# Down weights of a Strassen group stored by column half, loaded in four pieces instead of two

## The chip, the cores and the metric

The kernel runs on one core of a Trainium2 chip. The metric is the device time of one execution in microseconds (us); smaller is better. All arrays are float32, and TensorE multiplies them as fp32r (a float32 number cut into a high and a low part, three products for one).

## The reference

The reference is a trunk of two layers on 512 tokens of width 1024. Layer 0 mixes tokens by causal pooling, layer 1 by stick-breaking attention; each is followed by the MLP below, and every branch is wrapped in RMS norms. The change touches the second matrix of the MLP only, `w_down` (4096 x 1024).

```python
def sq_relu_mlp(h, w_up, w_down):
    u = jnp.matmul(h, w_up)
    return jnp.matmul(jnp.square(jax.nn.relu(u)), w_down)

for layer in range(DEPTH):                      # DEPTH = 2, D_FF = 4096
    ...                                         # mixer, residual
    h = rms_norm(x, mlp_pre_g[layer])
    x = x + rms_norm(sq_relu_mlp(h, w_up[layer], w_down[layer]), mlp_post_g[layer])
```

## The kernel before

**The MLP in blocks.** The 4096 hidden channels are 32 blocks of 128 (`NJ`). For each block the up projection (`up_block`, lines 764, 767 and 768: 24 matmuls of 512 columns) fills one PSUM bank; ScalarE takes relu and square of it into SBUF (`up`, lines 673 and 674). The weights of an up block come by DMA into a tile `raw`, are split by ScalarE into a high part (line 190) and by VectorE into a low part (line 192), up to four blocks ahead.

**The down projection by Strassen groups.** 28 of the 32 blocks go through the class `Seven`: five groups per layer with `GROUPS` = 2, 3, 3, 3, 3 pairs of blocks. A group multiplies 2x2 block matrices with seven products instead of eight. Its weights are four quarters: `w11`, `w12` (first block of each pair, output columns 0 to 511 and 512 to 1023) and `w21`, `w22` (second block of each pair). They are loaded unsplit: `w11` and `w12` lie in a tile `w1` (in the profile `w<-in_wdn`), `w21` and `w22` in `xn3`, a tile of three rows of 1024 that the norms use outside the MLP (in the profile `xn<-in_wdn`). For each product, `make(i)` builds the two operands: `left` forms sums of activations (line 593, tiles `r` and `s`), `right` forms sums of weight quarters (line 612), and both are split into high and low parts in tiles `a` and `w` (helper `split`: ScalarE line 312, VectorE line 313). The weight operands are, in order of the products 0 to 6:

- `w11`; then `w22 - w12` (tile `e`); then `e + w11`; then `w21 - e`; then `w12 - w11` (written over `w12`); then `w21`; then `w22`.

So the first sum of a group needs `w22` and `w12`, `w21` is not read before product 3, and the last reader of a group's `w22` is the split for its product 6.

**Order of the work.** Operands are made two products ahead: in the step of product i, `make(i + 2)` is called, and in the last two steps the coming group's products 0 and 1. One up block of the coming group follows each product on TensorE (line 638 is a product's matmul: 6 per pair, so 18 for a group of three pairs). A scheduler orders each engine's instructions by a timeline of its own at build time; each engine and the DMA queue of SP then run their list in order. In layer 0 SP also carries the weights of the attention: `split_apart` loads a block (`apart` or `spare`, line 243), ScalarE scales and splits it (lines 202 and 252), and both parts are written back to DRAM (`kept`, line 233).

**The loads.** `load(0)` and `load(1)` (line 577) fetch both quarters of one tile each. In DRAM `wdn` is block after block, 128 rows of 1024 each, so one load reads, for each of the 128 partitions, n rows of 4 KB that lie 1 MB apart, and writes them one after another into the partition.

Of the kernel before, what the change touches and what calls it, by code (L numbers as in the profile page):

```python
# [10 lines left out]
F32 = mybir.dt.float32  # L11
# [4 lines left out]
P = 128  # L16
D = 1024
# [4 lines left out]
NJ = FF // P  # L22
GRP = 4

GROUPS = (2, 3, 3, 3, 3)
MOST = max(GROUPS)
HEADS = 16
HD = 64
PAIRS = HEADS // 2
WINDOWS = (2, 4, 8, 16)  # L30
# [3 lines left out]
NS = [slice(0, 512), slice(512, 1024)]  # L34
# [90 lines left out]
def trunk(ctx, tc, x, bands, grow, pw, wup, wdn, wq, wk, wv, wo, out):  # L125
    nc = tc.nc
# [11 lines left out]
    def name(s):  # L138
        uid[0] += 1
        return f"{s}{uid[0]}"  # L140
# [14 lines left out]
    xn3 = work.tile([P, 3, D], F32, tag="xn3", name="xn3")  # L155
# [39 lines left out]
    def gains(lo, n):  # L195


        def scaled(raw):
            m = max(n, 4)
            for k in range(m):  # L200
                c, at = raw[:, k * D // m : (k + 1) * D // m], lo + k * n // m
                nc.scalar.mul(c, c, gc[:, at : at + 1])  # L202

        return scaled
# [3 lines left out]
    def want(key, src, scaled=None):  # L208
        queue.append((key, src, scaled))
# [16 lines left out]
    apart, kept, going = [], {}, []  # L226
# [52 lines left out]
    for l in range(2):  # L279
        if l == 1:  # L280
            n = len(queue)
            for what, i, part in ATT_ORDER:
                if what == "H" and not i and 0 in part:
                    for h in range(4):
                        want(("v", 0, h), wv[h], gains(C_KV * KC + 2 * h, 2))
                elif what == "V" and 0 in part:
                    for h in range(2):
                        want(("v", i, h), wv[2 * i + h], gains(C_KV * KC + 4 * h, 4))
                elif what == "K":
                    want(("k", i), wk[i], gains(C_KV * KC, KC))  # L290
                elif what in "PQ":
                    if ("k", i) not in [k for k, _, _ in queue]:
                        want(("k", i), wk[i], gains(C_KV * KC, KC))
                    want(("q", i), wq[i], gains(C_MIX_PRE1 * KC, KC))
                elif what == "O" and 0 in part or what == "E":
                    for c in range(2 * i, 2 * i + 2 if what == "O" else PAIRS):
                        want(("o", c), wo[c])
            asked = {x[0]: x for x in queue[n:]}
            for what in SPLIT_ORDER:
                key = (what[0], *(int(c) for c in what[1:]))  # L300
                apart.append(asked.pop(key))
            assert sorted(asked) == [("o", 0), ("o", 1)]

            queue[n - GRP : n + GRP] = queue[n : n + GRP - 1] + queue[n - GRP : n] + queue[n + GRP - 1 : n + GRP]
        for j in range(NJ):
            want(("up", l, j), wup[l, j])
        for j in range(NJ - GRP, NJ):
            want(("dn", l, j), wdn[l, j])


    def split(src, hi, lo):
        latest["act"] = nc.scalar.copy(hi, src)  # L312
        latest["dve"] = nc.vector.tensor_tensor(out=lo, in0=src, in1=hi.bitcast(F32), op=ALU.subtract)  # L313
# [160 lines left out]
    def need(*tiles):  # L474
        for t in tiles:
            if t in pending:
                pending.pop(t).transpose()
# [68 lines left out]
    class Seven:  # L546
# [19 lines left out]
            self.l, self.first, self.n, self.mp = l, first, n, mp  # L566
            self.banks, self.written, self.operands = {}, None, {}

        def load(self, second):

            n = self.n
            if second:
                w = self.w2 = xn3
            else:
                w = self.w1 = self.mp.tile([P, MOST, D], F32, tag="w1", name=name("w1"))
            src = wdn[self.l, self.first : self.first + 2 * n].rearrange("(n k) p d -> k p n d", k=2)
            nc.sync.dma_start(w[:, :n], src[1 if second else 0])

        def squares(self):
            self.r = self.mp.tile([P, 2, MOST, S], F32, tag="r", bufs=2, name=name("r"))  # L580

# [3 lines left out]
        def left(self, i):  # L585
# [4 lines left out]
            if i == 0:  # L590
                self.s1 = self.mp.tile([P, MOST, S // 2], F32, tag="s1", name=name("s1"))
            s1 = self.s1[:, :n]
# [7 lines left out]
            src = {"r11": r11, "s3": r21, "s2": r11, "r22": r22, "s1": s1, "r12": r12, "s4": r11}[key]  # L600
            a = self.mp.tile([P, 2, MOST, S // 2], F32R, tag="a", bufs=2, name=name("a"))
            split(src, a[:, 0, :n], a[:, 1, :n])
            return a

        def right(self, i):

            n, key = self.n, self.PRODUCTS[i][2]
            w11, w12, w21, w22 = (w[:, :n, h] for w in (self.w1, self.w2) for h in NS)
            if i == 0:
                self.e = self.mp.tile([P, MOST, 512], F32, tag="e", name=name("e"))  # L610
            e = self.e[:, :n]
            combine = lambda out, x, y, op=ALU.subtract: nc.vector.tensor_tensor(out=out, in0=x, in1=y, op=op)  # L612
            if key == "t3":
                combine(e, w22, w12)
            elif key == "t2":
                combine(e, e, w11, ALU.add)
            elif key == "t4":
                combine(e, w21, e)
            elif key == "t1":
                combine(w12, w12, w11)  # L620
            src = {"w11": w11, "t3": e, "t2": e, "t4": e, "t1": w12, "w21": w21, "w22": w22}[key]
            w = self.mp.tile([P, 2, MOST, 512], F32R, tag="w", bufs=2, name=name("w"))
            split(src, w[:, 0, :n], w[:, 1, :n])
            return w
# [24 lines left out]
    def mlp(l, mp, update):  # L649
# [5 lines left out]
        groups = [Seven(l, firsts[g], n, mp) for g, n in enumerate(GROUPS)]  # L655
# [27 lines left out]
                squares.append((a[:, 0], a[:, 1]))  # L683

        entering = dict(normed_by)
        groups[0].load(0)
        groups[0].squares()
        if l == 0:
            apart_hi[0] = wts.tile([P, 2, D], F32R, tag="wx", name=name("wx"))
# [5 lines left out]
        for j, (pu, w) in enumerate(first):  # L695
            if j == n0 - 1:
                need(2, 3)
                groups[0].load(1)
            if j >= len(early):
                up_block(pu, w, slice(0, S // 2))  # L700
        early.clear()
# [8 lines left out]
        for g, group in enumerate(groups):  # L710
            coming = groups[g + 1] if g + 1 < len(groups) else None
            if coming:
                coming.squares()
            ups = list(range(firsts[g + 1], firsts[g + 1] + 2 * GROUPS[g + 1]) if coming else range(plain, NJ))
            if g == 0:
                up(ups.pop(0))
                fill()
            else:
                with tc.issue_after(latest["dve"].ins):
                    while entering:  # L720
                        entering.popitem()[1].homogeneous_eps()
            for i in range(7):
                group.product(i, y, written if g == 0 else None)
                if 7 * g + i in steps:
                    with tc.issue_after(latest["act"].ins), tc.issue_after(latest["dve"].ins):
                        split_apart(mp)
                if ups:
                    up(ups.pop(0))
                if i + 2 < 7:
                    group.make(i + 2)  # L730
                    if i + 2 == 4 and coming:
                        coming.load(0)
                    if i + 2 == 6 and coming:
                        coming.load(1)
                elif coming:
                    coming.make(i + 2 - 7)
                elif i == 5:
                    piece = lambda tag, k, bufs=1: mp.tile([P, k, D], F32R, tag=tag, bufs=bufs, name=name("dn"))
                    w, e, x = piece("w1", 3), piece("e", 1), piece("w", 3, 2)
                    c = piece("apart", 1, 3)[:, 0]  # L740
                    dn_raw["dn", l, NJ - 2] = mp.tile([P, D], F32, tag="apart", bufs=3, name=name("dn"))
                    dn_raw["dn", l, NJ - 1] = mp.tile([P, D], F32, tag="apart", bufs=3, name=name("dn"))
                    dn_pool[0] = [[w[:, 0], w[:, 1]], [w[:, 2], e[:, 0]], [c, x[:, 2]], [x[:, 0], x[:, 1]]]

                if l == 0:
                    behind.update(latest)
                fill(1 + (coming is None and i == 6))
# [3 lines left out]
        w = [get(("dn", l, j)) for j in range(plain, NJ)]  # L751
# [24 lines left out]
    with tc.tile_pool(name="mix0", bufs=1, reuse_waits="tile") as mp:  # L776
# [6 lines left out]
        half = NW * BW // 2  # L783
# [9 lines left out]
        at = D + P + 4 * KC  # L793
# [16 lines left out]
        left, stats, ups, ys, own = {}, {}, {}, {}, {}  # L810
# [146 lines left out]
    with tc.tile_pool(name="att", bufs=1, reuse_waits="tile") as ap:  # L957
# [68 lines left out]
        half = [slice(0, HD), slice(HD, P)]  # L1026
# [20 lines left out]
        with tc.issue_after(latest["pool"].ins):  # L1047
            nc.gpsimd.memset(begin, 0.0)
            for lo, n in SEG.values():
                c = min(n - P, 1)  # L1050
                d = begin[:, lo + n - P - c : lo + n]
# [320 lines left out]
    return np.concatenate([packed, *first], axis=1).astype(np.float32)  # L1372


# [43 lines left out]
```

## Time and profile before

The columns of a row of instruction groups on the profile's page are: line, engine, operation, output<-inputs, shape, count | busy time, mean of one | idle time before it and what ended it.

| what | before |
|---|---|
| median of three runs | 899.36 us (897.89, 899.36, 899.59) |
| the profiled execution | 899.84 us, of which 898.1 us are the profiled span |
| TensorE busy | 888.9 us (99% of the span) |
| VectorE, ScalarE busy | 690.4 us (77%), 555.6 us (62%) |
| granted TensorE clock, mean | 0.998 |
| loads of a group of three pairs (1.5 MB), layer 0, issue to landing | 7.8 to 11.2 us |
| the same, layer 1 | 6.7 to 7.1 us |

A matmul's row shows 0.38 us for 512 columns, but the next one starts 0.22 us later: they are pipelined, so TensorE is at its pace when the starts follow each other at 0.22 us. Idle time of an engine costs nothing unless it delays TensorE, which is what the span is made of.

### The profile page before, as it was taken

To read this page: it belongs to the slowest core of one execution; us is meant where nothing else is said; L and a number is where in the kernel's file an instruction comes from. 1 tells how busy PE (TensorE), PEld (TensorE's weight loads), DVE (VectorE), ACT (ScalarE), POOL (GpSimd) and SP (SyncE) were. 2 spreads that over 40 slices of the span, in tenths; PEclk is the share of its full clock that TensorE was granted. 3 is DMA by queue.
4 is the path that set the end of the run, shared out by engine and by line. 5 is a ranking of instruction groups with operands and counts; after the bars stand their busy time and mean duration, and the time that the engine had idled before them with its cause. 6 is when DMAs were issued, how large, how long until landed. Compare 5 with 4: busy or idle time off the path is not lost.

```text
span 898.1 us, 12323 instructions
## 1 busy us (share of the span) xinstructions
PE 888.9 (99%) x4688; PEld 786.5 (88%) x4688; DVE 690.4 (77%) x800; ACT 555.6 (62%) x984; POOL 37.8 (4%) x78
## 2 busy tenths in 40 slices
PE   9999999999999999999999999999999999999997
PEld 6998888888888888888999888998888888888886
DVE  6876799998988977268777478884696976968866
ACT  6667679898796947256455464875545444444632
POOL 3200000000000004000000000200000000000002
PEclk9999999999999999999999999999999999999999
DMA  8446969889698750643152272442514233133002
GB/s 303 147 148 217 344 233 340 326 277 410 220 342 285 285 189 2 209 166 134 56 187 93 95 281 71 153 176 96 186 40 164 79 140 117 47 141 118 24 1 94
DMA packets 42685, 155.73 MB, mean 173 GB/s; under 512 B 4225, under 2 KB 4353, under 8 KB 42626
## 3 DMA queue, kind: packets, MB, share of 16 engines
q1 hardware_dynamic: 42624, 154.94, 47.9%
q8 instruction: 37, 0.61, 0.3%
q14 instruction: 22, 0.18, 0.1%
q10 hardware_dynamic: 2, 0.00, 0.0%
HBM read 121.38 MB, written 33.55 MB: 173 GB/s over the span
## 4 chain that ended last, share of the span: by engine, by line
PE 87%; DVE 4%; DMA 4%; ACT 3%; issue 2%; POOL 0%; SPq 0%; POOLq 0%; ACTq 0%; DVEq 0%
PE ps L638 24%; PE ps L767 14%; PE ps L764 14%; PE ps L768 14%; PE ps L331 4%; PE ps L333 4%; PE ps L332 4%; DMA xn<-in_wdn 2%; PE ps L1133 2%; PE ps L1114 2%; PE ps L1158 2%; PE ps L903 1%; PE ps L438 1%; DVE w L313 1%; DMA x<-in_x 1%
## 5 line engine op out<-in xcount | busy, mean ns | idle before, releaser
L638 PE MATMUL ps<-w,a 128*128 128x512 f32 x1176 | 266.3, 379 | 0.7 <-ACT a L312 0.7
L767 PE MATMUL ps<-xnh,w 128*128 128x512 f32 (+1 forms) x704 | 253.4, 362 | 0.0
L768 PE MATMUL ps<-xnl,w 128*128 128x512 f32 (+1 forms) x704 | 252.8, 360 | 0.0
L764 PE MATMUL ps<-xnh,w 128*128 128x512 f32 (+1 forms) x704 | 252.2, 360 | 0.3 <-DVE w L924 0.3
L638 PEld LDWEIGHTS ps<-w,a 128*128 128x128 f32 x1176 | 222.0, 189 | 32.9 <-ACT a L312 1.1
L764 PEld LDWEIGHTS ps<-xnh,w 128*128 128x128 f32 x704 | 132.9, 190 | 15.9 <-DVE w L924 0.4
L768 PEld LDWEIGHTS ps<-xnl,w 128*128 128x128 f32 x704 | 133.5, 190 | 15.2
L767 PEld LDWEIGHTS ps<-xnh,w 128*128 128x128 f32 x704 | 133.0, 190 | 15.3
L192 DVE TENSOR_TENSOR w<-raw,w 128x1024 fp32r<-128x1024 f32 x58 | 70.8, 1221 | 48.4 <-ACT w L190 48.4
L190 ACT CAST w<-raw 128x1024 fp32r<-128x1024 f32 x58 | 60.6, 1044 | 69.2 <-PE ps L764 68.2
L647 DVE TENSOR_TENSOR y<-ps,y 128x512 f32<-128x512 f32 x124 | 83.7, 684 | 24.5 <-PE ps L638 24.2
L312 ACT CAST a<-r 128x768 fp32r<-128x768 f32 (+1 forms) x60 | 47.4, 790 | 56.0 <-PE ps L638 36.5
L312 ACT CAST w<-e 128x1536 fp32r<-128x1536 f32 (+1 forms) x30 | 41.8, 1392 | 34.3 <-DVE e L612 26.2
L313 DVE TENSOR_TENSOR a<-r,a 128x768 fp32r<-128x768 f32 (+1 forms) x60 | 53.9, 898 | 8.3 <-ACT a L312 8.3
L1095 DVE TENSOR_TENSOR_SCAN e<-u,begin 128x1280 f32<-128x1280 f32 x16 | 45.2, 2825 | 18.6 <-ACT u L1079 17.9
L313 DVE TENSOR_TENSOR w<-e,w 128x1536 fp32r<-128x1536 f32 (+1 forms) x30 | 49.3, 1644 | 0.7 <-ACT w L312 0.5
L202 ACT ACTIVATE apart<-apart,eye 128x128 f32<-128x128 f32 (+1 forms) x128 | 42.4, 409 | 0.0
L313 DVE TENSOR_TENSOR w<-w,w 128x1536 fp32r<-128x1536 f32 (+1 forms) x20 | 33.0, 1648 | 4.7 <-ACT w L312 4.7
L674 ACT ACTIVATE r<-r 128x512 f32<-128x512 f32 x56 | 35.3, 630 | 1.3
L313 DVE TENSOR_TENSOR w<-xn,w 128x1536 fp32r<-128x1536 f32 (+1 forms) x20 | 33.0, 1649 | 3.7 <-ACT w L312 3.3
L673 ACT ACTIVATE r<-ps 128x512 f32<-128x512 f32 x56 | 33.1, 591 | 3.9 <-PE ps L764 3.9
L312 ACT CAST w<-w 128x1536 fp32r<-128x1536 f32 (+1 forms) x20 | 27.7, 1385 | 5.9 <-DMA w<-in_wdn 5.9
(148 smaller groups left out, 1293.4 us busy)
## 6 DMA issues: line engine op xcount, KB each, us to landing
raw<-in_wup SPq DMA_DIRECT2D x64, 512.0 KB, 3.8
w<-kept SPq DMA_DIRECT2D x60, 512.0 KB, 4.3
kept<-wx SPq DMA_DIRECT2D x30, 512.0 KB, 5.2
kept<-apart SPq DMA_DIRECT2D x24, 512.0 KB, 5.9
w<-in_wdn SPq DMA_DIRECT2D x8, 1536.0 KB, 7.4
xn<-in_wdn SPq DMA_DIRECT2D x8, 1536.0 KB, 8.3
apart<-in_wq SPq DMA_DIRECT2D x7, 512.0 KB, 6.9
kept<-spare SPq DMA_DIRECT2D x6, 512.0 KB, 6.0
```

What stands on the lines that cost most here:

```text
L190: nc.scalar.copy(hi, raw)
L192: nc.vector.tensor_tensor(out=lo, in0=raw, in1=hi.bitcast(F32), op=ALU.subtract)
L202: nc.scalar.mul(c, c, gc[:, at : at + 1])
L312: latest["act"] = nc.scalar.copy(hi, src)
L313: latest["dve"] = nc.vector.tensor_tensor(out=lo, in0=src, in1=hi.bitcast(F32), op=ALU.subtract)
L331: nc.tensor.matmul(dst, ah, bh, start=start, stop=False)
L638: nc.tensor.matmul(bank, a[:, x, q, TS[t]], woven(w[:, z, q], NS[0]), start=start and q == 0 and k == 0, stop=q == self.n - 1 and k == 2, ...
L647: nc.vector.tensor_tensor(out=part, in0=bank, in1=part, op=ALU.add)
L764: nc.tensor.matmul(pu[:, cols], wl[:, k, :], moving(xnh, k), start=False, stop=k == KC - 1)
L767: nc.tensor.matmul(pu[:, cols], wh[:, k, :], moving(xnh, k), start=k == 0, stop=False)
L768: nc.tensor.matmul(pu[:, cols], wh[:, k, :], moving(xnl, k), start=False, stop=False)
L1095: nc.vector.tensor_tensor_scan(out=self.e[:, ::-1], data0=self.u[:, 1:][:, ::-1], data1=begin[:, ::-1], initial=0.0, op0=ALU.mult, op1=ALU ...
```

## The change

`wdn` is stored group by group as a flat array: for each group first `w11` of all its pairs, then `w12`, `w21`, `w22`; in each quarter the partition is outermost, so a partition's share of a quarter is n x 512 numbers in one piece (6 KB for three pairs, 4 KB for two), and a quarter of a group of three pairs is one piece of 0.75 MB. The two SBUF tiles get the same order: half 0 is numbers 0 to 1535 of a partition, half 1 is 1536 to 3071. `load(second, half)` fetches one quarter. The loads are asked for after the `make` of the steps 2, 3, 4 and 5: `w11`, `w12`, `w22`, `w21`. What is computed, and with which operations, is the same.

```diff
+LOADS = {2: (0, 0), 3: (0, 1), 4: (1, 1), 5: (1, 0)}
...
-        def load(self, second):
+        def load(self, second, half):
             n = self.n
             if second:
-                w = self.w2 = xn3
-            else:
-                w = self.w1 = self.mp.tile([P, MOST, D], F32, tag="w1", name=name("w1"))
-            src = wdn[self.l, self.first : self.first + 2 * n].rearrange("(n k) p d -> k p n d", k=2)
-            nc.sync.dma_start(w[:, :n], src[1 if second else 0])
+                self.w2 = xn3.rearrange("p n d -> p (n d)").rearrange("p (h n c) -> p h n c", h=2, n=MOST)
+            elif not half:
+                self.w1 = self.mp.tile([P, 2, MOST, 512], F32, tag="w1", name=name("w1"))
+            size = P * n * 512
+            src = wdn[self.l, self.first * P * D + (2 * second + half) * size :][: size]
+            w = self.w2 if second else self.w1
+            nc.sync.dma_start(w[:, half, :n], src.rearrange("(p n c) -> p n c", p=P, n=n))
...
-            w11, w12, w21, w22 = (w[:, :n, h] for w in (self.w1, self.w2) for h in NS)
+            w11, w12, w21, w22 = (w[:, h, :n] for w in (self.w1, self.w2) for h in range(2))
...
-        groups[0].load(0)
+        groups[0].load(0, 0)
+        groups[0].load(0, 1)
...
-                groups[0].load(1)
+                groups[0].load(1, 1)
+                groups[0].load(1, 0)
...
-                    if i + 2 == 4 and coming:
-                        coming.load(0)
-                    if i + 2 == 6 and coming:
-                        coming.load(1)
...
+                if coming and i in LOADS:
+                    coming.load(*LOADS[i])
```

The first place is SP's queue in layer 0 around the loads of the third group (`w<-in_wdn` and `xn<-in_wdn`). Before:

```order
L577 DMA w_1289<-in_wdn 128x3x1024
L233 DMA kept_1389<-wx_526 128x1024
L233 DMA kept_1389<-apart_1172 128x1024
L243 DMA spare_1392<-in_wk 128x1024
L180 DMA raw_1435<-in_wup 128x1024
L233 DMA kept_1461<-wx_526 128x1024
L233 DMA kept_1461<-apart_1243 128x1024
L243 DMA apart_1464<-in_wq 128x1024
L233 DMA kept_1536<-wx_526 128x1024
L577 DMA xn_78<-in_wdn 128x3x1024
```

And now:

```order
L580 DMA w_1293<-in_wdn 128x1536 x2
L234 DMA kept_1394<-wx_527 128x1024
L234 DMA kept_1394<-apart_1176 128x1024
L244 DMA spare_1397<-in_wk 128x1024
L181 DMA raw_1440<-in_wup 128x1024
L234 DMA kept_1466<-wx_527 128x1024
L580 DMA xn_78<-in_wdn 128x1536
L234 DMA kept_1466<-apart_1247 128x1024
L244 DMA apart_1469<-in_wq 128x1024
L234 DMA kept_1542<-wx_527 128x1024
L580 DMA xn_78<-in_wdn 128x1536
```

The two halves of `w1` stand one behind the other where the one load stood. Of the two `xn` rows the first writes numbers 0 to 1535 of the tile, which is `w21`, and the second `w22`: the scheduler has turned the order of the source around, since `w21` comes free a step earlier. `w22` stands where the whole load stood; `w21` has moved ahead of `kept<-apart`, `apart<-in_wq` and `kept<-wx`. From the second group of a layer on, every group has this order; in the first group of layer 1 too, in that of layer 0 `w22` stands first.

The second place is VectorE in layer 1 at the change from the first group to the second. Before (first row: the split of the first group's `w22`; `e<-xn,w` is `w22 - w12` of the second group, `w<-w` alone is `w12 - w11`, `w<-w,w` the low part of `w11`, `y<-ps` the addition of a finished product):

```order
L313 TENSOR_TENSOR w_6089<-xn_78,w_6089 128x1024
L192 TENSOR_TENSOR w_6040<-raw_6041,w_6040 128x1024
L647 TENSOR_TENSOR y_5644<-ps_6098,y_5644 128x512
L593 TENSOR_TENSOR s_6114<-r_5794 128x768
L647 TENSOR_TENSOR y_5645<-ps_6099,y_5645 128x512
L612 TENSOR_TENSOR e_6118<-xn_78,w_5986 128x1536
L313 TENSOR_TENSOR a_6115<-r_5794,a_6115 128x768
L593 TENSOR_TENSOR r_5794<-r_5794 128x3x256
L313 TENSOR_TENSOR w_6119<-w_5986,w_6119 128x1536
L612 TENSOR_TENSOR w_5986<-w_5986 128x3x512
L313 TENSOR_TENSOR w_6143<-e_6118,w_6143 128x1536
```

And now:

```order
L314 TENSOR_TENSOR w_6102<-xn_78,w_6102 128x1024
L615 TENSOR_TENSOR e_6131<-xn_78,w_5998 128x1536
L193 TENSOR_TENSOR w_6053<-raw_6054,w_6053 128x1024
L650 TENSOR_TENSOR y_5654<-ps_6111,y_5654 128x512
L596 TENSOR_TENSOR s_6127<-r_5806 128x768
L650 TENSOR_TENSOR y_5655<-ps_6112,y_5655 128x512
L615 TENSOR_TENSOR w_5998<-w_5998 128x1536
L314 TENSOR_TENSOR a_6128<-r_5806,a_6128 128x768
L314 TENSOR_TENSOR w_6132<-w_5998,w_6132 128x1536
L596 TENSOR_TENSOR r_5806<-r_5806 128x3x256
L314 TENSOR_TENSOR w_6157<-e_6131,w_6157 128x1536
```

`e<-xn,w` has moved up, ahead of the up block's split, both `y` and `s`; `w<-w` has moved ahead of `a` and of the low part of `w11`.

The third place is TensorE at the same change of groups: the last matmuls of an up block and what follows them (`w_6119` and `w_6132` are the operand of the second group's product 0, `w_6143` and `w_6157` that of its product 1; two matmuls of product 0 have run ahead of the up block in both kernels). Before:

```order
L767 MATMUL ps_6185<-xnh,w_5933 128x512
L768 MATMUL ps_6185<-xnl,w_5933 128x512
L764 MATMUL ps_6185<-xnh,w_5933 128x512
L638 MATMUL ps_6224<-w_6143,a_6139 128x512
L638 MATMUL ps_6225<-w_6143,a_6139 128x512
L767 MATMUL ps_6246<-xnh,w_5988 128x512
```

And now:

```order
L770 MATMUL ps_6199<-xnh,w_5945 128x512
L771 MATMUL ps_6199<-xnl,w_5945 128x512
L767 MATMUL ps_6199<-xnh,w_5945 128x512
L641 MATMUL ps_6177<-w_6132,a_6128 128x512 x8
L641 MATMUL ps_6178<-w_6132,a_6128 128x512 x8
L641 MATMUL ps_6238<-w_6157,a_6153 128x512 x2
```

Before, product 1's first two matmuls and 11 matmuls of the next up block came between the up block and the other 16 matmuls of product 0; now these 16 follow the up block at once. In layer 0 the order of TensorE's rows is the same in both kernels, and that of VectorE and ScalarE too behind the first group.

More of the change, by code (lines that the diff above doesn't have):

```diff
@@ L307, in trunk @@
         for j in range(NJ - GRP, NJ):
-            want(("dn", l, j), wdn[l, j])
+            want(("dn", l, j), wdn[l, j * P * D : (j + 1) * P * D].rearrange("(p d) -> p d", p=P))
     def split(src, hi, lo):
@@ L1372, in pooling_bands, with grouped @@
     return np.concatenate([packed, *first], axis=1).astype(np.float32)
+def grouped(w):
+    w, parts, at = w.reshape(2, NJ, P, 2, 512), [], 0
+    for n in GROUPS:
+        own = w[:, at : at + 2 * n].reshape(2, n, 2, P, 2, 512)
+        parts.append(own.transpose(0, 2, 4, 3, 1, 5).reshape(2, -1))
+        at += 2 * n
+    return np.concatenate([*parts, w[:, at:].reshape(2, -1)], 1)
 def kernel(x, pool_w, pool_scale, w_q, w_kv, kv_norm_g, w_o, w_up, w_down,
@@ L1400 @@
         "wup": np.stack([blocks(w, P).reshape(NJ, P, D) for w in a["w_up"]]),
-        "wdn": apart(a["w_down"]).reshape(2, NJ, P, D),
+        "wdn": grouped(apart(a["w_down"])),
         "wq": blocks(a["w_q"][0], P).reshape(PAIRS, P, D),
```

## The prediction

> **What bounds the kernel now.** I read the page first, then who makes TensorE wait, then stretches of the span.
>
> ```profile
> span 898.1 us, 12323 instructions
> PE 888.9 (99%) x4688; PEld 786.5 (88%) x4688; DVE 690.4 (77%) x800; ACT 555.6 (62%) x984; POOL 37.8 (4%) x78
> L638 PE MATMUL ps<-w,a 128*128 128x512 f32 x1176 | 266.3, 379 | 0.7 <-ACT a L312 0.7
> ```
> ```profile
> PE ps L638 <- ACT a L312: 0.7, 1, 0.7
> PE ps L764 <- DVE w L924: 0.3, 1, 0.3
> PE ps L875 <- DVE own L863: 0.3, 1, 0.3
> ```
> ```profile
> 60.00:330.00 270.00, 269.32 (x1248) 235.28 (x1247) 234.82 (x239) 213.24 (x354) 0.00 (x0) 1.00 0.80 291
> 603.00:850.00 247.00, 247.00 (x1146) 216.25 (x1145) 187.15 (x191) 127.94 (x152) 0.00 (x0) 1.00 0.30 106
> ```
>
> The columns of the last two rows are stretch, length, busy time of PE, PEld, DVE, ACT and POOL (instructions), granted clock, DMA share, GB/s. TensorE sets the time. In the 247 us of layer 1's MLP it is never idle, in the 270 us of layer 0's MLP for 0.68 us, at one place, where it waits for ScalarE's high part of an `a`. The number of matmuls does not change. So the loads, which the change speeds up, can win at most that one stall; everything else they make faster is off the path. VectorE (235 of 270 us) and the DMA (80%) are close behind TensorE in layer 0, and there a wait is passed on soonest.
>
> **The one stall and its chain.** TensorE's matmuls, ScalarE, VectorE:
>
> ```profile
> 171.78 0.38 PE L764 MATMUL ps<-xnh,w 128*128 128x512 f32 x1
> 172.83 0.48 PE L638 MATMUL ps<-w,a 128*128 128x512 f32 x1 [0.68 <-ACT a L312]
> ```
> ```profile
> 153.06 1.28 ACT L202 ACTIVATE spare<-spare,eye 128x128 f32<-128x128 f32 x4 [0.74 <-DMA spare<-in_wk]
> ...
> 171.95 0.83 ACT L312 CAST a<-r 128x768 fp32r<-128x768 f32 x1 [2.72 <-DVE r L593]
> ```
> ```profile
> 158.85 1.76 DVE L313 TENSOR_TENSOR w<-w,w 128x1536 fp32r<-128x1536 f32 x1 [1.72 <-ACT w L312]
> ...
> 162.53 0.68 DVE L647 TENSOR_TENSOR y<-ps,y 128x512 f32<-128x512 f32 x1
> 163.35 1.76 DVE L612 TENSOR_TENSOR e<-xn,w 128x1536 f32<-128x1536 f32 x1
> ```
>
> Starts lie 0.22 us apart when TensorE flows, so this stall costs 172.83 - 171.78 - 0.22 = 0.83 us. Followed back: the high part waited for VectorE's `r`; VectorE had worked without a gap since 158.85 (except 0.14 us before 163.35, when it waited for the `xn` load); at 158.85 it had waited for ScalarE, and ScalarE had lost 0.74 us because `spare<-in_wk` had not landed. That load stands in SP's queue behind the 1.5 MB load of `w1`.
>
> **Term 1, layer 0: the loads run faster.** Pace of the DMA in stretches (last two numbers: DMA share, GB/s): the first is filled with pieces of 0.5 MB, the others with the old 1.5 MB loads of 4 KB rows 1 MB apart.
>
> ```profile
> 92.00:98.00 6.00, 6.00 (x30) 5.25 (x29) 4.93 (x6) 4.59 (x6) 0.00 (x0) 1.00 1.03 421
> 101.00:108.00 7.00, 7.00 (x34) 6.09 (x33) 6.45 (x7) 5.70 (x8) 0.00 (x0) 1.00 0.96 342
> 642.00:646.40 4.40, 4.40 (x22) 3.84 (x22) 2.45 (x3) 3.11 (x5) 0.00 (x0) 1.00 0.91 345
> ```
>
> A quarter is now one piece of 0.75 MB like the 0.5 MB ones, only longer. At 421 instead of 343 GB/s the two halves of `w1` (1.57 million bytes) take 3.74 instead of 4.59 us, so what stands behind them lands 0.85 us earlier, and ScalarE's 0.74 us go. `w22` must follow: its half lands behind w21's half and the same other pieces as before, so also 0.85 us earlier, in time for an `e` that starts 0.74 us earlier. The chain moves as a whole and the stall shrinks to 0.1 us: gain 0.74 us. Bounds: 0 (pace stays at 343, or another wait takes over) and 0.83, since a stall can't give more than itself. I take 0.74, because the 421 row is of the same kind of piece. `w21`'s half, moved ahead of `kept`, `apart` and `kept`, delays those by 0.79 MB / 421 = 1.87 us less the 0.85 us; ScalarE's only DMA wait in this layer was the one above, so the others have room, at least for this 1.0 us.
>
> **Term 2, layer 1, first change of groups: `e` is moved ahead.** SP's issue of `w21` and `w22`, VectorE behind it, TensorE:
>
> ```profile
> 640.59 0.38 SPq L577 DMA_DIRECT2D xn<-in_wdn  x1
> ```
> ```profile
> 643.95 1.23 DVE L192 TENSOR_TENSOR w<-raw,w 128x1024 fp32r<-128x1024 f32 x1 [3.44 <-ACT w L190]
> 645.10 0.68 DVE L647 TENSOR_TENSOR y<-ps,y 128x512 f32<-128x512 f32 x1
> 645.70 0.95 DVE L593 TENSOR_TENSOR s<-r 128x768 f32<-128x768 f32 x1
> 646.56 0.68 DVE L647 TENSOR_TENSOR y<-ps,y 128x512 f32<-128x512 f32 x1
> 647.44 1.76 DVE L612 TENSOR_TENSOR e<-xn,w 128x1536 f32<-128x1536 f32 x1 [0.20 <-DMA xn<-in_wdn]
> 649.12 0.95 DVE L313 TENSOR_TENSOR a<-r,a 128x768 fp32r<-128x768 f32 x1
> 649.99 0.95 DVE L593 TENSOR_TENSOR r<-r 128x768 f32<-128x768 f32 x1
> 650.86 1.75 DVE L313 TENSOR_TENSOR w<-w,w 128x1536 fp32r<-128x1536 f32 x1
> 652.52 1.75 DVE L612 TENSOR_TENSOR w<-w 128x1536 f32<-128x1536 f32 x1
> 654.19 1.75 DVE L313 TENSOR_TENSOR w<-e,w 128x1536 fp32r<-128x1536 f32 x1
> ```
> ```profile
> 653.47 0.59 PE L638 MATMUL ps<-w,a 128*128 128x512 f32 x2
> ...
> 656.27 4.05 PE L638 MATMUL ps<-w,a 128*128 128x512 f32 x18
> ```
>
> Before, product 0's other 16 matmuls (in the x18) came at 656.27, and the low part they need (650.86 + 1.75) was done at 652.61. Now they come right behind the up block, at 653.47, and on VectorE the low part stands behind `e`, the up split, `y`, `s`, `y`, `w<-w` and `a`. From start to start in the rows: 1.68 + 1.15 + 0.60 + 0.86 + 0.60 + 1.67 + 0.87, and 1.75 for itself: 9.18 us after `e` starts. So `e` has to start by 644.29. It waits for `w22`, whose load can't be issued before 640.59, since it overwrites the `w22` of the first group, read until then. How long 0.75 MB take is in no row; 0.5 MB (the `raw` loads from 600 to 680) and 1.5 MB (the `wdn` loads of layer 1) are:
>
> ```profile
> DMA to landing us min/median/max: 3.3/3.5/4.5
> ...
> DMA to landing us min/median/max: 6.7/6.8/7.1
> ```
>
> From 0.5 MB up at 421 GB/s: 3.5 + 0.6 = 4.1 us; on the line between both rows 4.3; the ends are 3.9 (3.3 + 0.6) and 6.7 (as long as the whole). I take 4.1: landing 644.7, start 644.8 (0.1 from landing to start, as at 647.44), low part done at 653.97, TensorE waits 0.5 us. With 3.9 it is 0.3 us, with 6.7 it is 3.2 us. Behind `e` on VectorE wait the up split, whose block TensorE reaches two blocks later, and the two `y` and `s`, which all end before the low part, so that a wait for them would be inside this one. Product 1's low part follows `r` (0.87) and ends 2.5 us after product 0's, while product 0's matmuls take 16 x 0.22 = 3.5 us: no second stall.
>
> The Trainium skill (DMA: Bandwidth & Descriptors, Anatomy of one DMA) has 2.0 us plus bytes / 436e3 per DMA, on another issue path; by that a half would take 3.8 us, the wait would be 0.2 us and the sum 0.3 us lower.
>
> **No cost elsewhere.** At layer 1's later changes of groups TensorE has room:
>
> ```profile
> 699.03 1.76 DVE L612 TENSOR_TENSOR e<-xn,w 128x1536 f32<-128x1536 f32 x1 [1.07 <-DMA xn<-in_wdn]
> ...
> 701.58 1.75 DVE L313 TENSOR_TENSOR w<-w,w 128x1536 fp32r<-128x1536 f32 x1
> ```
> ```profile
> 702.24 7.93 PE L638 MATMUL ps<-w,a 128*128 128x512 f32 x36
> ```
>
> The low part was done at 703.33, product 0 (the second 18 of the 36) began at 702.24 + 18 x 0.216 = 706.13: 2.8 us of room. The new order puts `y` (0.6) and `w<-w` (1.67) ahead of it, the load gives back the 1.07 us wait and more: still over 1.6 us. In the first group of layer 1, `w22`'s half now covers a row of `xn3` that the last token tile's transposes read:
>
> ```profile
> 584.10 1.29 PE L438 MATMUL ps<-eye,xn 128*128 128x128 f32 x8
> ```
> ```profile
> 588.85 1.21 DVE L612 TENSOR_TENSOR e<-xn,w 128x1024 f32<-128x1024 f32 x1
> ...
> 597.35 1.23 DVE L192 TENSOR_TENSOR w<-raw,w 128x1024 fp32r<-128x1024 f32 x1 [1.61 <-ACT w L190]
> ```
>
> So SP holds it, and two weight loads behind it, until 585.2; 3.5 us later is 588.7, just in time for `e` at 588.85. If it comes 1 us late, VectorE's idle 1.61 us take it up. The 20 more issues cost SP 0.38 us each (the row at 640.59), spread over the two MLPs; what stands behind them comes 0.4 us later, and of ScalarE's casts only the one at 153.06 waited for a load in layer 0. The sums and splits have the same sizes; contiguous halves change nothing, as `w<-w,w` (strided) and `w<-e,w` (contiguous) both take 1.75 us above.
>
> **Sum.** -0.74 + 0.5 = -0.24 us. Against the profiled execution's 899.84 that is 899.6; the median of the runs is 0.48 lower, so 899.1. The runs of one kernel spread over 1.7 us (0.19%), so about 0.2% (1.8 us) is what can be told from no change.
>
> **Rivals.**
> - *The half is no quicker than the whole (slower).* If `w22`'s half lands after 6.7 us, the wait at 653.47 is 3.2 us: net +2.4, 901.8. It decides against the kernel from a landing of about 6.1 us on (stall 2.6, less 0.74). For it: no row has a 0.75 MB piece, and single 0.5 MB loads took up to 4.5 us; against: their median of 3.5 and the one stream that is in flight then. Chance 0.09.
> - *More and smaller loads clog layer 0 (slower or even).* A 0.5 MB load takes 3.5 us alone and 1.25 us of moving, so 2.25 us are fixed; if the second half of `w1` pays that again, `spare` lands later, ScalarE's wait grows and the stall with it: +2.25 + 0.5, 902.1. The row at 421 GB/s, all pieces of 0.5 MB, speaks against it: in a full queue the fixed part is hidden. Chance 0.05. The Trainium skill (same page, Bandwidth) advises loads of at least 1 MiB; that rule would have it so, the 421 row does not agree.
> - *Only the gain.* `w22` lands within 3.6 us of its issue, so that `e` starts by 644.29: -0.74, 898.6. For it: 3.3 us were seen for 0.5 MB; against: the 0.6 us that 0.25 MB more take at 421 GB/s. Chance 0.16.
> - *The pace does not change.* 6 KB rows move at 343 GB/s, the old stall stays and the new one comes: 899.36 + 0.5 = 899.9, still no change. Chance 0.16.
> - *A gain over 0.2%.* TensorE has no 1.8 us to win; only scatter. Chance 0.05.
>
> My own case has the rest, 0.49; its own range is 898.5 to 900. Together: faster 0.05, within 0.2% 0.82 (with a part of the borderline cases), slower 0.13. The range: from 898.6 less half the runs' spread, 897.7, up to 901.2, which leaves out the two slower cases.
>
> **What would show it.** Right: TensorE's stall near 172 gone or near 0.1 us; a new wait of TensorE of some 0.5 us at 653, on VectorE's `w` of line 314, right behind an up block; loads of 0.75 MB in layer 1 landing in about 4.1 us; no VectorE wait for `xn` at the later changes of groups. Wrong: TensorE's waits in the two MLPs adding up to over 1.5 us, or a stall near 600.

## The result, and the profile after

The changed kernel takes 901.02 us (median of 16 runs, 899.62 to 902.73), the kernel before 899.34 us (16 runs, 897.89 to 900.55). The ratio is 1.0017, with a 95% interval of 1.0009 to 1.0025: slower by 1.5 us by the ratio and 1.7 by the medians, where a gain of 0.24 us was forecast. The page of the changed kernel and TensorE's list of waits:

```profile
span 899.9 us, 12364 instructions
...
PE 888.0 (99%) x4688; PEld 786.0 (87%) x4688; DVE 691.3 (77%) x800; ACT 555.2 (62%) x984; POOL 37.9 (4%) x78
```
```profile
PE ps L439 <- ACT xn L429: 1.6, 1, 1.6
...
PE ps L641 <- DVE w L314: 0.7, 1, 0.7
```

The stall near 172 is gone from the list (a start-to-start excess of 0.11 us is left of 0.84), the forecast stall at 653 is there, and a third one, on ScalarE's `xn` of line 429, is new and was not forecast. TensorE's matmuls come in the same order in both kernels up to 653, so they can be set side by side one by one: the changed kernel gains 0.74 us at 172, loses 1.60 us at 585 and 0.97 us at 655, and nothing else after the first 10 us. Together that is +1.83 us; the two spans differ by 1.8 us.

**The stall that was not forecast.** SP's queue, ScalarE and TensorE of the changed kernel, at the end of layer 1's mixer:

```profile
570.69 0.33 SPq L580 DMA_DIRECT2D xn<-in_wdn  x1
572.03 0.33 SPq L1275 DMA_DIRECT2D raw<-in_wup  x1
572.45 0.86 SPq L580 DMA_DIRECT2D w<-in_wdn  x2
```
```profile
578.73 1.07 ACT L1279 CAST w<-raw 128x1024 fp32r<-128x1024 f32 x1 [1.31 <-DMA raw<-in_wup]
...
583.82 1.04 ACT L1279 CAST w<-raw 128x1024 fp32r<-128x1024 f32 x1 [1.16 <-DMA raw<-in_wup]
584.77 0.72 ACT L429 ACTIVATE xn<-x,stat 128x512 f32<-128x512 f32 x1
```
```profile
585.54 0.66 PE L439 MATMUL ps<-eye,xn 128*128 128x128 f32 x4 [1.62 <-ACT xn L429]
```

The first row is w21's half of layer 1's first group (0.5 MB). Before, both quarters of that tile were one load, issued at 579.07, behind the up weights; the half now covers only a row that comes free earlier, and stands 1.34 us ahead of the first up weights `raw`. In the kernel before ScalarE had no such waits, though next to no room either: the second `raw` landed at 582.88 and its cast started at 583.02.

```profile
583.02 1.03 ACT L1276 CAST w<-raw 128x1024 fp32r<-128x1024 f32 x1
583.96 0.72 ACT L428 ACTIVATE xn<-x,stat 128x512 f32<-128x512 f32 x1
```

The landing of that `raw` load (issued at 572.80 before and at 572.03 after), from its issue, before and after:

```profile
DMA to landing us min/median/max: 3.7/3.7/3.7
```
```profile
DMA to landing us min/median/max: 6.6/6.6/6.6
```

ScalarE's order is fixed, so the late cast holds up the last token tile's norm (`xn`, line 429), and TensorE the four transposes that read it.

**The stall that was forecast.** VectorE and TensorE of the changed kernel at layer 1's first change of groups:

```profile
645.92 1.76 DVE L615 TENSOR_TENSOR e<-xn,w 128x1536 f32<-128x1536 f32 x1 [4.59 <-DMA xn<-in_wdn]
647.60 1.22 DVE L193 TENSOR_TENSOR w<-raw,w 128x1024 fp32r<-128x1024 f32 x1
...
653.33 1.75 DVE L314 TENSOR_TENSOR w<-w,w 128x1536 fp32r<-128x1536 f32 x1
```
```profile
654.06 0.38 PE L767 MATMUL ps<-xnh,w 128*128 128x512 f32 x1
655.14 1.56 PE L641 MATMUL ps<-w,a 128*128 128x512 f32 x6 [0.70 <-DVE w L314]
```

`e` starts when w22's half lands, the low part ends 9.16 us later at 655.08, and TensorE starts at 655.14.

### The profile page after: what moved, and what is told of

It is laid out like the page before. It is cut to its first block, busy times and chain, and to the rows that moved or that the text cites. A ratio compares the mean times of both kernels' runs of the same rounds, so it can differ in the third digit from the quotient of the medians.

```text
span 899.9 us, 12364 instructions
## 1 busy us (share of the span) xinstructions
PE 888.0 (99%) x4688; PEld 786.0 (87%) x4688; DVE 691.3 (77%) x800; ACT 555.2 (62%) x984; POOL 37.9 (4%) x78
## 4 chain that ended last, share of the span: by engine, by line
PE 92%; DVE 3%; DMA 2%; ACT 1%; issue 1%; POOL 0%; SPq 0%; POOLq 0%; ACTq 0%; DVEq 0%
PE ps L641 28%; PE ps L770 15%; PE ps L767 15%; PE ps L771 15%; PE ps L332 4%; PE ps L334 4%; PE ps L333 4%; PE ps L1136 2%; PE ps L1117 2%; PE ps L1161 2%; PE ps L906 1%; DMA raw<-in_wup 1%; PE ps L878 1%; DMA x<-in_x 1%; PE ps L439 1%
## 5 line engine op out<-in xcount | busy, mean ns | idle before, releaser
L321 POOL TENSOR_SCALAR stat<-stat,eps 128x1 f32<-128x1 f32 x8 | 5.4, 680 | 605.6 <-ACT xn L317 605.6
```

## The experiments

Executions differ: in the first 10 us, ahead of everything that the change touches, TensorE's 29th matmul started between 8.7 and 10.4 us in the seventeen traces taken. That spread is as large as the effects, so the times alone tell little, and the traces decide. The table has, per trace, what TensorE lost at the three places (start to start, less what it is when TensorE flows; at 655 with the 0.10 us that the second matmul waits, while the same 0.10 us behind a stall at 172 are left out; at 584 the kernel before always shows 0.20), the landing of layer 1's first up weights, and how late VectorE's `e` of layer 0's third group (near 163) starts: its distance from a TensorE matmul near 106 us, less 56.13 us, the one constant chosen to fit.

| kernel | 172 | 584 | 655 | landing of `raw` | `e` near 163 late by |
|---|---|---|---|---|---|
| before, four traces | 0.84, 0, 1.06, 1.00 | 0.20 each | 0 each | 3.67, 3.81, 3.71, 3.66 | 0.84, -0.34, 1.06, 1.00 |
| changed, four traces | 0.11, 0, 0.27, 1.42 | 1.78, 0.90, 1.32, 1.80 | 0.96, 0.76, 0.66, 0.70 | 6.60, 5.71, 6.09, 6.57 | 0.10, -0.25, 0.27, 1.42 |
| w21 late in layer 1 | 0 | 0.20 | 0.77 | 3.70 | -0.05 |
| `e` late in layer 1 | 0 | 0.91 | 0 | 5.72 | -0.17 |
| both | 0.33 | 0.35 | 0 | 3.93 | 0.32 |
| rows of 2 KB | 1.56 | 1.29 | 1.06 | 5.45 | 1.57 |
| half of w21 early | 0.43 | 0.54 | 1.18 | 4.00 | 0.43 |
| before, rows of 12 KB | 1.18 | 0.39 | 0 | 3.92 | 1.19 |
| both, and w22 first in layer 0, three traces | 0, 0, 0 | 0.20, 0.19, 0.20 | 0 each | 3.85, 3.69, 3.70 | -0.34, -0.72, -0.32 |

**1. w21's half of layer 1's first group behind w22's.**

```diff
...
-                groups[0].load(1, 1)
-                groups[0].load(1, 0)
+                last = groups[0].load(1, 1)
+                with tc.issue_after(last.ins) if l == 1 else nullcontext():
+                    groups[0].load(1, 0)
```

> The changed kernel, but in layer 1's first group w21's half is issued behind w22's half, where the whole load stood before; nothing else moves. Theory (the queue): the 1.6 us stall at 584 comes from w21's 0.5 MB, which stand ahead of the up block's `raw` loads in SP's queue, so that ScalarE's two casts wait 1.3 and 1.2 us and the last token tile's norm comes late. Then both casts start without a wait on `raw`, the stall is gone and the time falls by 1.6 us, to about 0.3 us over the kernel before (899.6). Rival 1 (slow transfers): the up block's load is slow at 574 to 578 because of the smaller pieces around it, wherever w21 stands; then at least half of the stall stays, 900.3 or more. Rival 2 (the hold): SP waits for the last token tile's transposes before w22's half, as the prediction had it, and that sets the time; then nothing changes, 901.0.

Measured: 899.98 us, ratio 1.0006 (0.9994 to 1.0018). TensorE's waits in the MLPs are now one, and the up weights land as before the change:

```profile
PE ps L641 <- DVE w L314: 0.5, 1, 0.5
```
```profile
DMA to landing us min/median/max: 3.7/3.7/3.7
```

The stall at 584 is back at the 0.20 us of the kernel before. The queue order is its cause: the first rival would have kept at least half of it, the second all of it. The time decides nothing: the ratio is 0.5 us over the kernel before, with an interval from -0.5 to +1.6 us, and holds both the theory (0.3) and the first rival (1.0 or more).

**2. `e` behind the up split and one `y`.** `added` records the additions of finished products.

```diff
             if key == "t3":
-                combine(e, w22, w12)
+                with tc.issue_after(added[1, 0, 5, 0].ins) if (self.l, self.first) == (1, 2 * GROUPS[0]) else nullcontext():
+                    combine(e, w22, w12)
...
```

> The changed kernel, but at layer 1's first change of groups VectorE's `e` (w22 - w12) stands behind the up split and one `y`, which do not need the new load, instead of ahead of them; TensorE, ScalarE and SP keep their order. Theory (the order on VectorE): `e` waits 4.6 us for w22's half, and the low part that TensorE needs at 653 stands behind it with 9.2 us of work; with 1.7 us of this work done inside the wait, the low part ends about 1.7 us earlier, the 0.7 to 0.9 us stall at 655 is gone and the time falls by 0.9 to 1.0 us, to about 900.1. Rival (the load alone): `e` waits for the load wherever it stands and all behind it keeps its time; then 901.0, unchanged.

Measured: 899.20 us, ratio 1.0005 (0.9996 to 1.0013). VectorE of this kernel:

```profile
644.36 0.68 DVE L651 TENSOR_TENSOR y<-ps,y 128x512 f32<-128x512 f32 x1
644.97 1.75 DVE L615 TENSOR_TENSOR e<-xn,w 128x1536 f32<-128x1536 f32 x1
...
650.63 1.75 DVE L314 TENSOR_TENSOR w<-w,w 128x1536 fp32r<-128x1536 f32 x1
```

The low part starts 5.66 us after `e` instead of 7.41, `e` waits for nothing, and the stall at 655 is 0. The load took 4.3 us, as in the changed kernel, so the order on VectorE made the stall, not the load alone. The time is 0.9 us under the expected 900.1, which the interval (up to 900.5, from 899.34) still holds; here too it decides less than the trace. The stall at 584 is there, at 0.91: it varies from execution to execution.

**3. Both edits.** The two diffs above together.

> Both edits at once: w21 of layer 1's first group behind w22, and `e` behind the up split and one `y` at layer 1's first change of groups. If the two new stalls are all that the change costs, only the gain in layer 0 (0.7 us) is left: 0.7 us under the kernel before, about 898.6 (ratio 0.9992). If another wait is behind one of them, or the gain in layer 0 is lost further down, the time is that of the kernel before or above, 899.3 or more.

Measured: 899.46 us, ratio 1.0004 (0.9995 to 1.0012). The expected 0.9992 lies below the interval: the two stalls are gone, except for 0.15 us at 584, and still a gain of 0.7 us did not appear. TensorE's list of waits:

```profile
PE ps L439 <- ACT xn L429: 0.2, 1, 0.2
PE ps L642 <- ACT a L313: 0.2, 1, 0.2
```

The last row is the stall at 172, here 0.33 us. That put the gain in layer 0 in doubt.

**4. Rows of 2 KB.** A quarter lies pair by pair in DRAM; all engines and SP's queue keep their order.

```diff
-            nc.sync.dma_start(w[:, half, :n], src.rearrange("(p n c) -> p n c", p=P, n=n))
+            nc.sync.dma_start(w[:, half, :n], src.rearrange("(n p c) -> p n c", p=P, n=n))
...
-        parts.append(own.transpose(0, 2, 4, 3, 1, 5).reshape(2, -1))
+        parts.append(own.transpose(0, 2, 4, 1, 3, 5).reshape(2, -1))
```

> The changed kernel with the same four loads per group in the same order on every engine and queue, but a quarter lies pair by pair in DRAM, so that a load has rows of 2 KB, 256 KB apart, instead of 6 KB in one piece. Theory (row length sets the pace): the two quarters of w1 in layer 0 move no faster than the old loads (343 GB/s or less against 421), the stall at 172 comes back (0.8 us or more) and w22's half at 641 takes 0.4 us or more longer, which adds that to the stall at 655: 1.1 us or more over the changed kernel, 902.1 or more. Rival (the size of a piece): quarters move fast because they are smaller loads, whatever their rows; then no stall at 172 and 901.0.

Measured: 900.98 us, ratio 1.0024 (1.0014 to 1.0033), by the ratio between the two expectations, with an interval that holds both. A stall of 1.56 us at 172 came, but the changed kernel itself has 1.42 in one of four traces, so it decides nothing. What stands alone is a load: w22's half of layer 0's second group, 0.75 MB in a full queue, landed after 7.2 us here and after 6.3 to 6.6 us in all eleven traces with rows of 6 KB. These rows of the two kernels, 2 KB first:

```profile
DMA to landing us min/median/max: 7.2/7.2/7.2
```
```profile
DMA to landing us min/median/max: 6.5/6.5/6.5
```

So rows of 2 KB cost 0.7 us on such a load, in the one trace there is; that it sets the stall isn't shown. The pace that the theory expected, 343 GB/s or less, did not come. These rows have stretch, length, busy times, clock, DMA share and GB/s, the rows of 2 KB first, then the changed kernel:

```profile
101.00:108.00 7.00, 7.00 (x34) 6.09 (x33) 7.00 (x8) 4.85 (x6) 0.00 (x0) 1.00 1.00 396
```
```profile
101.00:108.00 7.00, 7.00 (x34) 6.09 (x33) 7.00 (x8) 5.64 (x8) 0.00 (x0) 1.00 1.02 415
```

The kernel before has 342 GB/s there. And w22's half at 641, expected to take 0.4 us or more longer, landed after 4.5 us, against 4.1 to 4.4.

**5. Both kernels once more.** No edit.

> The kernel before once more, for a second trace of it. If its one stall in layer 0 belongs to the kernel, TensorE waits 0.7 us for ScalarE's `a` at 172 again, has no wait at 584 or 653, and the first up weights of layer 1 land within 4 us; the ratio is 1. If the stall at 172 was scatter of that one execution, it is absent or at another place, and the gain of 0.7 us that the comparison showed is not the change's.

> The changed kernel once more, for a second trace of it. If the stalls belong to the change, TensorE waits at 584 (0.7 to 1.6 us, as in the three traces that have w21's half ahead of the up weights) and at 655 (0.6 to 0.9 us), not at 172 (0.2 us at most), and the ratio is about 1.0017. If the 1.6 us was scatter of one execution, the wait at 584 is under 0.5 us and the ratio nearer to 1.0009.

Measured: the kernel before against itself 1.0006 (0.9995 to 1.0018), the changed one 900.82 us, 1.0014 (1.0005 to 1.0023). The changed kernel's two stalls are there again. But the second trace of the kernel before has no stall at 172. The prediction tied that stall to ScalarE's wait for `spare`. ScalarE and VectorE of the second trace:

```profile
151.76 1.28 ACT L202 ACTIVATE spare<-spare,eye 128x128 f32<-128x128 f32 x4 [0.85 <-DMA spare<-in_wk]
```
```profile
107.22 1.75 DVE L612 TENSOR_TENSOR e<-xn,w 128x1536 f32<-128x1536 f32 x1
...
162.02 1.76 DVE L612 TENSOR_TENSOR e<-xn,w 128x1536 f32<-128x1536 f32 x1
```

The wait for `spare` is longer than in the first trace (0.74), and no stall follows. In the first trace there is this instead, 64 us ahead of the stall:

```profile
108.63 1.76 DVE L612 TENSOR_TENSOR e<-xn,w 128x1536 f32<-128x1536 f32 x1 [1.18 <-DMA xn<-in_wdn]
```

VectorE starts this `e` 1.41 us later than in the second trace (1.26 with TensorE's own shift of 0.15 taken off), and the `e` at 163.35 is still 1.33 us later. Between these two sums VectorE idles 3.8 us in either trace, but most of that in waits for ScalarE, whose own instructions wait for VectorE's sums and start up to 1.42 us later too. The two engines pass the lag back and forth, and one late load is carried 64 us until TensorE waits for it.

**6. Half of w21 early in layer 1.** One pair of w21 ahead of the up weights, the other behind w22; the third argument of `load` picks the pair.

```diff
...
-                groups[0].load(1, 1)
-                groups[0].load(1, 0)
+                last = groups[0].load(1, 1)
+                if l == 1:
+                    groups[0].load(1, 0, 0)
+                with tc.issue_after(last.ins) if l == 1 else nullcontext():
+                    groups[0].load(1, 0, 1 if l == 1 else None)
```

> The changed kernel, but only half of w21's load of layer 1's first group (0.25 MB, one pair) stands ahead of the up weights in SP's queue, the rest behind w22. Without it they landed 3.7 to 3.9 us after issue, behind the whole 0.5 MB after 5.5 to 6.6 us. Theory (bytes ahead in the queue): about half the difference, landing after 4.6 to 5.3 us, and a stall at 584 of 0.2 to 0.8 us. Rival (the presence of a load ahead, whatever its size): 5.5 us or more and a stall of 0.7 us or more.

Measured in one execution: `raw` landed after 4.0 us, the stall at 584 is 0.54 us, 0.34 over the kernel before. Fewer bytes ahead give a smaller stall, against the rival; the landing came below the range that the theory gave, so the delay doesn't go with the bytes in proportion. Two things besides the bytes differ: the piece has rows of 2 KB instead of 4 KB, and `raw` was issued 1.77 us behind it instead of 1.34.

**7. The kernel before with rows of 12 KB.** Both loads of a group stay whole and the order on all engines and queues is unchanged; a group's weights lie in DRAM as each load reads them.

```diff
-            src = wdn[self.l, self.first : self.first + 2 * n].rearrange("(n k) p d -> k p n d", k=2)
-            nc.sync.dma_start(w[:, :n], src[1 if second else 0])
+            size = P * n * D
+            src = wdn[self.l, self.first * P * D + second * size :][: size]
+            nc.sync.dma_start(w[:, :n], src.rearrange("(p n d) -> p n d", p=P, n=n))
```

> The kernel before, with its two whole loads per group and the same order on every engine and queue; only the down weights of a group lie in DRAM as each load reads them, so that a load has rows of 12 KB in one piece instead of 4 KB, 1 MB apart. Theory (rows set the pace, as in Term 1): loads of w1 move at about 420 instead of 343 GB/s, the stall at 172 shrinks to 0.2 us or less, no wait appears at 584 or 653, since no load changes its place, and the time falls by 0.7 us to a ratio of 0.9992. Rival (the smaller pieces set the pace): the loads stay at 343 GB/s, the stall at 172 stays at 0.7 us and the ratio is 1.

Measured: 898.66 us, ratio 0.9994 (0.9985 to 1.0003), unclear between the two. The load at 97 took 9.0 us against 9.5 to 11.2 us in the four traces of the kernel before, and the loads of 1.5 MB in layer 1 took 6.4 to 6.6 against 6.7 to 7.2 us, so long rows are somewhat quicker; yet the stall at 172 is 1.18 us, with `e` near 163 late. The pace at 101 to 108 is not the 420 GB/s of the theory:

```profile
101.00:108.00 7.00, 7.00 (x34) 6.09 (x33) 7.00 (x8) 5.09 (x7) 0.00 (x0) 1.00 0.97 359
```

The four traces of the kernel before have 342 to 358. So in this stretch halves with rows of 2 KB go faster (396) than whole loads with rows of 12 KB (359): the length of the rows does not set the pace there, by one trace of each. Whether the size of the loads or their order in the queue does, no run here separates.

**8. Two more traces of each kernel.**

> A third trace of the kernel before. Between its first two traces VectorE differs by one step alone: in the first it waits 1.2 us at 108.6 for layer 0's load of `xn`, in the second not, and from there on it stays 1.3 us apart until TensorE waits 0.8 us, or not at all, at 172. Theory (scatter of the landing): the stall at 172 is there when VectorE's first sum `e` with the loaded `xn` near 108 or near 163 waits for the load by about 1 us or more, and absent otherwise; this trace shows one of the two. Rival (spare, as the prediction had it): the stall follows ScalarE's wait for `spare` near 152, whatever the two sums do.

> A fourth trace of the kernel before, with the same question: a stall at 172 with a late `xn` at 108 or 163 (theory), or with ScalarE's wait for `spare` at 152 (rival). If the stall is there in half of the traces or fewer, the change's gain in layer 0 is 0.4 us or less on average.

> A third trace of the changed kernel. The first two have stalls of 1.6 and 0.7 us at 584, of 0.9 and 0.7 us at 655 and none over 0.1 us at 172. If these are the change's, this trace has 0.5 to 1.7 us at 584, 0.6 to 1.1 us at 655, and at 172 no more than 0.3 us.

> A fourth trace of the changed kernel, with the same ranges: 0.5 to 1.7 us at 584, 0.6 to 1.1 us at 655, at most 0.3 us at 172.

Measured: the kernel before has the stall in both, 1.06 and 1.00 us. The changed kernel has its two new stalls in both, and one of them has 1.42 us at 172, beyond what was expected. VectorE and TensorE of that execution (span 901.3 us):

```profile
164.22 1.76 DVE L615 TENSOR_TENSOR e<-xn,w 128x1536 f32<-128x1536 f32 x1 [1.35 <-DMA xn<-in_wdn]
```
```profile
173.70 0.48 PE L641 MATMUL ps<-w,a 128*128 128x512 f32 x1 [1.26 <-ACT a L313]
```

Now the table's last column says what the stall at 172 is: in all seventeen traces it equals, to 0.02 us, how late `e` near 163 starts, and is 0 where `e` is early. Waits for `spare` don't go with it (1.3 us in experiment 1, no stall). In every trace with a stall but the first, `e` itself waits there for `xn`, by 0.5 to 1.6 us.

**9. w22 first in layer 0.** Experiment 3, and in layer 0's third group w21's half behind w22's; `e` is held to its old place, so that only that one load moves in SP's queue.

```diff
-                combine(e, w22, w12)
+                after = {(1, 4): (1, 0, 5, 0), (0, 10): (0, 4, 6, 0)}.get((self.l, self.first))
+                with tc.issue_after(added[after].ins) if after else nullcontext():
+                    combine(e, w22, w12)
...
-                    coming.load(*LOADS[i])
+                    with tc.issue_after(last.ins) if i == 5 and (l, g) == (0, 1) else nullcontext():
+                        done = coming.load(*LOADS[i])
+                    if i == 4:
+                        last = done
```

> Both earlier edits, and in layer 0's third group w21's half is issued right behind w22's instead of three pieces of 0.5 MB ahead of it; every engine's order is that of the kernel with both edits. In the traces so far the stall at 172 equals how late VectorE's `e` near 163 starts, to 0.02 us. Theory (the queue sets that landing): with 0.79 MB less ahead, w22's half lands about 2 us earlier after its issue (8.6 to 9.9 us instead of 10.6 to 11.9), `e` does not wait, and no stall at 172 is left, nor one over 0.4 us at 584 or 655; 0.3 us less than with both edits alone, about 0.7 us under the kernel before (ratio 0.999). Rival (the stall has another cause further up, the late landing only goes with it): `e` starts no earlier and the stall is between 0 and 1.4 us as before.

> A second trace of the same kernel. Theory: no stall at 172 here either. Rival: a stall in about two of three traces, as in the four of the kernel before (0.8, 0, 1.1, 1.0 us).

> A third trace of the same kernel. Theory: no stall at 172. Rival: a stall in about two of three traces.

Measured: 898.95 us, ratio 0.9996 (0.9987 to 1.0005); the two further executions 898.92 and 898.43 us. VectorE and the landing of w22's half of the first of the three:

```profile
161.81 1.75 DVE L615 TENSOR_TENSOR e<-xn,w 128x1536 f32<-128x1536 f32 x1
```
```profile
DMA to landing us min/median/max: 9.8/9.8/9.8
```

In all three `e` doesn't wait (the half lands 0.45 to 0.50 us before `e` starts), and no stall is left at 172, 584 (over the usual 0.20) or 655. That supports the theory: what stands ahead of w22 in the queue sets the stall. It is not proof, since three of the eight traces with w21's half ahead have no stall either. The half landed after 9.8, 9.4 and 9.8 us, against 10.2 to 11.9 us in the eight traces that have w21's half ahead in rows of 6 KB: 1.1 us earlier on average, not 2 us. This kernel is faster than the changed one (0.9996 against 1.0017 and 1.0014, intervals that at most touch); that it also beats the kernel before is likely by the traces, but the interval holds 1.

## Why the prediction was wrong

**The step that failed: "No cost elsewhere", the first group of layer 1.** It followed w22's half only, and asked whether that comes in time for `e` ("So SP holds it, and two weight loads behind it, until 585.2"). It did: `e` has no wait there in any of the changed kernel's four traces. What it did not follow is the other half of the same tile, though the order of the queue was known to have w21's half first there. Splitting the load frees w21's half from the last row's readers, the scheduler issues it 1.3 us ahead of the up weights, and behind these stand ScalarE's casts and the last norm. Cost, as the mean of four traces: 1.45 - 0.20 = 1.25 us, forecast as nothing. The prediction itself counted such a shift in layer 0 ("`w21`'s half, moved ahead") and left it out here, where ScalarE had 0.14 us of room (582.88 to 583.02). With the stall came the prediction's own sign of being wrong: waits of 1.62 + 0.70 = 2.3 us, where it named over 1.5.

**Term 2 (forecast 0.5 us) was right in its mechanism and too small.** Place, waiting engine and the 9.18 us from `e` to the low part's end came out (9.16). The halves of `xn` in layer 1 landed after:

```profile
DMA to landing us min/median/max: 4.1/4.2/4.4
```

4.1 us was taken, and the one that counts took 4.4 in the first trace and 4.1 to 4.2 in the other three. With the second matmul's wait the stall is 0.66 to 0.96, 0.77 us on average. The Trainium skill (DMA: Bandwidth & Descriptors, Anatomy of one DMA) gives 2.0 us plus bytes / 436e3 for DMAs that GpSimd issues, an estimate of 3.8 us for a half; the rows, of loads that SyncE issues, don't agree, and they decide.

**Term 1 (forecast -0.74 us) came out to 0.01 us in the first pair of traces by luck.** Its chain was followed back to `spare` and no further. VectorE's lag was older: it came from the wait for `xn` at 108.6, of that execution alone. Nor did the halves of `w1` remove the wait for `spare`: it is 0.74, 0.85, 0.96 and 0.96 us in the four traces before and 0.24, 0.56, 1.09 and 1.37 us after. The pace behind the term fails too. From 142 to 149 us, where `w1`'s loads move, the DMA has 303 to 347 GB/s in the four traces before and 329 to 362 after, not 421. And 343 GB/s was not the pace of rows of 4 KB as such: in the same trace of the kernel before, with the whole load of `xn` (issued at 153.21, landed at 163.33) in flight, the DMA is as fast as with pieces of 0.5 MB:

```profile
160.00:163.00 3.00, 3.00 (x16) 2.62 (x15) 3.00 (x4) 3.00 (x10) 0.00 (x0) 1.00 1.03 416
```

Over four traces each, the stall is 0.73 us before and 0.45 us after, so the term measures -0.28 us. Experiments 1, 2, 3 and 6 leave layer 0 as it is in the changed kernel; with them the mean after is 0.32 us over eight traces. A gain of 0.3 to 0.4 us is thus likely, but with stalls from 0 to 1.1 us before and from 0 to 1.4 us after it isn't certain.

**The sum.** By the means of four traces: -0.28 + 1.25 + 0.77 = +1.74 us; the medians of the runs differ by 1.68 us. That 901.0 us lies within the stated 897.7 to 901.2 is luck as well: it lies outside the 898.5 to 900 of the prediction's own case, and the largest term was not in the sum. At the later changes of groups in layer 1 TensorE lost nothing, as forecast. `e`, forecast without a wait, waits 0.3 us there instead of 1.1:

```profile
698.36 1.76 DVE L615 TENSOR_TENSOR e<-xn,w 128x1536 f32<-128x1536 f32 x1 [0.29 <-DMA xn<-in_wdn]
```

Of the rivals none was it. "The half is no quicker than the whole" has a time close to the measured one (901.8), but the half was quicker, 4.2 against 6.8 us; the loads did not clog layer 0 (the wait for `spare` is 0.8 us on average, against 0.9 before); and "the pace does not change" is right about the pace of `w1`'s loads, but leaves out the new stall at 584. What was wrong in the working is that a single trace's stall was taken for the kernel's, and that of two new loads only the later one was traced through the queue.

## What to carry to other kernels

When a load is split, follow each piece through the queue: a piece that depends on less is issued earlier, and everything that used to stand ahead of it now stands behind it. Follow a stall back past the last visible wait, to the point from which the engine is late, and look at a second execution before counting on its removal. A pace read in one stretch is that stretch's: see whether the same loads go faster in another. A wait moved into an engine's list is paid by what stands behind it; filling it with two instructions that need nothing new took it away.

## What was not expected of the hardware

On SP's queue near 572 the first load of a burst, where it has 0.5 MB, landed 3.5 to 3.9 us after its issue. In the changed kernel's four traces and in experiment 2, which have w21's half first and `raw` second, each from the third on landed 1.3 us behind the one ahead. The second took longer: `raw` landed 3.5 to 4.5 us behind the first, though it was issued only 1.3 us later. So in this place 0.5 MB ahead cost 1.9 to 2.9 us of landing (5.7 to 6.6 against 3.7 to 3.8), more than the 1.3 us of its bytes. The DMA was busy meanwhile, but slow; first the kernel before, then the changed one:

```profile
574.50:576.50 2.00, 2.00 (x17) 1.92 (x16) 2.00 (x6) 2.00 (x6) 0.55 (x1) 1.00 1.03 397
```
```profile
574.50:576.50 2.00, 2.00 (x21) 2.00 (x20) 2.00 (x5) 2.00 (x6) 0.55 (x1) 1.00 0.88 244
```

From 2 to 4 us after `raw`'s issue it moved 373 to 403 GB/s in the four traces before and 229 to 307 in the four after. Why it is slow there, and why the delay varies from one execution to the next, stays open.
